# A decoder step on one core: decode strips queued as sets, keys before values in the projections, the convolution's norm earlier

## The chip, the cores and the metric

The kernel runs on one core of one Trainium2 chip. The time is the device time of one execution in microseconds (us). TensorE (PE) multiplies matrices, VectorE (DVE) and ScalarE (ACT) do elementwise work, GpSimd (POOL) too; SyncE (SP) issues every DMA. Each engine takes its instructions in order.

## What is computed

The reference runs one inference step of a trunk of two layers for a prompt of 1024 tokens and a sample group of 8 sequences with 4 new tokens each. The first layer mixes by differential attention (4 heads) beside a causal depthwise convolution of width 31, the second by a diagonal state-space scan; a squared-ReLU MLP stands behind each. Only the first layer's mixer is touched:

```python
def even_mixer(xn, w_in, lam_qk, subln_g, conv_w, conv_b, ln_g, ln_b, w_out, layer, k_past, v_past, conv_buf):
    q, k, v, ug = jnp.split(xn @ w_in, [A_Q_W, 2 * A_Q_W, 2 * A_Q_W + A_V_W], axis=-1)
...
    attn = rms_norm(attn, subln_g, SUBLN_EPS) * (1.0 - lam_init)
    a, g = jnp.split(ug, 2, axis=-1)
    u = a * jax.nn.sigmoid(g)
    c, new_buf = causal_depthwise_conv(u, conv_buf, conv_w, conv_b)
    c = jax.nn.silu(layer_norm(c, ln_g, ln_b))
    mixed = jnp.concatenate([attn.reshape(bt, L, A_V_W), c], axis=-1)
    return mixed @ w_out, k, v, new_buf
```

The prompt attends to itself. The sample group attends to 2048 cached tokens per sequence, in pages of 128 that a page table names, and to its own 4.

## The kernel before, in words

Activations lie with features on the 128 partitions and the 1056 tokens (1024 of the prompt, 32 new) on the free axis, as slabs of 128x1056 from a pool of 48; a pool of PSUM banks takes the products. Float32 operands are split in a high and a low part, and a product of 128x352 is three matmuls (L195 to L197). The code is emitted in program order with a scheduler behind it that sets each engine's order; DMAs keep the order of the program (`dma`, L96), on SP's one queue.

`mixer0` (L1488) computes 20 units of 128 features of the input projection in the order `seq` (L1491), `part` for a third of the tokens and `whole` (L1559) at the end of a unit: gates and conv inputs, queries, at the end values (8 to 11), then keys (4 to 7). Queries and keys are written to DRAM (`qd`, `kd`) and come back per head (`head_load`, L1281); `head_split` makes their high and low parts. `tokens` (L1475) transposes keys and values to tokens on the partitions, for the outputs and, values only, for `vd`, from which each head's values (`v`) are loaded.

Then `prompt` (L1431) runs 32 blocks, 4 heads by 8 blocks of 128 queries: scores (`sp`, L1324 to L1327), softmax in pieces (`pst`, `p`), transposed weights (`wT`, L1386), and with values (`av`, L1401). At block TH (24) it starts `conv_half`.

Beside this main line run generators, kept in `bg` and advanced by `pump` at given rates as the main line is emitted:

- `decode_k` (L1126) loads key pages (`pg`), transposes them (`kT`, L1142) and multiplies them with the new tokens' queries in *strips*: products of 32 rows that lie side by side on TensorE, one for each of 4 sequences (s) and 4 heads (h) (`strips`, `sc`, L1154). After 64 pages it waits for the new keys (`kready`), scores them and gives the group g (0 or 1) to `dec_softmax` (L1244), whose weights are transposed (`pT`).
- `decode_v` (L1191) loads value pages and multiplies, again in strips, four sequences side by side (`O`, L1217).
- `convs` (L981) computes the convolution on VectorE, 31 steps for each of 4 slabs (L977), and writes each slab (`acc`) to `cd`.
- `conv_norm` (L1037) runs when the projections have ended: it loads the four slabs, subtracts the mean over the 512 channels, sums squares, and multiplies by the root (`rows_rsqrt`, L1022: ScalarE's Abs_reciprocal_sqrt, `cs`); then Silu, and back to `cd`.
- `conv_half` (L1078) loads these (`cz`), splits them (`zh`, `zl`) and computes the conv half of the out-projection: 24 products of 12 matmuls.

Behind the last block the rest of `conv_half` and the attention's half of the out-projection follow (`finish`: `aT`, transposed heads; then `product`).

## Time and profile before

| | |
|---|---|
| runs | 2707.85, 2715.56, 2710.91 us; median 2710.91 |
| profiled execution | 2710.83 us, its span 2709.1 us |
| mean granted clock of TensorE | .967 |
| busy: PE, DVE, ACT, POOL | 2524.2, 1709.3, 1016.9, 738.3 us |
| projections of the first layer | 127 to 334 us |
| attention, blocks 1 to 20 | 333.7 to 496.8 us |
| attention, blocks 21 to 32 | 496.8 to 587.8 us |
| last score to `product` | 587.8 to 658.5 us |

Times are counted from the span's start. The profile is of one execution: the page gives sums over the whole span, in which TensorE is busy 93%; what a change in one stretch is worth is read from the rows of that stretch alone, in windows, waits (what ended an engine's idle time), groups of instructions, and the timeline. A matmul on 256 or 512 columns in float32 strips leaves two records. Ends of matmuls are modelled and overlap, so the time of one is read from its start to the next start.

### The profile page before, as it was taken

The page shows a single profiled execution, that of the slowest core. Times are in us where ns is not written, and L with a number is a line of the kernel's source. Part 1 is how long each engine was busy: PE and PEld are TensorE (multiplying, and loading weights), DVE is VectorE, ACT ScalarE, POOL GpSimd, SP SyncE. Part 2 cuts the span into 40 slices and gives each one's busy share as a digit, 9 for nine tenths or more (in the row PEclk, how much of TensorE's full clock was granted, in tenths as well). Part 3 has the DMA queues.
Part 4 walks back from the last instruction along what each step waited for, and adds up shares of the span by engine and source line. Part 5 has one row for each costly group of instructions (what it writes and reads, how often), then busy time and mean ns, then how long its engine had stood idle before and what let it go on. Part 6 is the DMA issues. An engine that isn't in the chain of part 4 may idle for free. (4 is left out here: it accounts for less than half of the span.)

```text
span 2709.1 us, 42679 instructions
## 1 busy us (share of the span) xinstructions
PE 2524.2 (93%) x16315; PEld 2392.4 (88%) x16315; DVE 1709.3 (63%) x3036; ACT 1016.9 (38%) x2034; POOL 738.3 (27%) x1090
## 2 busy tenths in 40 slices
PE   8999979789899999999999787799879999999998
PEld 7999855559799999999999776699779999999997
DVE  6777666763868554655545999951686767455435
ACT  6133345754441222222213466642552333412103
POOL 0110001112616875343402588710510000000004
PEclk9999989999999999999999899899889999999999
DMA  5353689663032223222222433213032233433221
GB/s 187 93 170 112 202 269 318 188 222 106 14 113 63 91 82 96 61 79 82 90 78 67 168 111 111 67 35 125 22 128 95 96 116 132 174 95 110 87 80 65
DMA packets 240868, 311.41 MB, mean 115 GB/s; under 512 B 27604, under 2 KB 168162, under 8 KB 240655
## 3 DMA queue, kind: packets, MB, share of 16 engines
q1 hardware_dynamic: 240331, 308.44, 35.3%
q8 instruction: 129, 2.11, 0.3%
q14 instruction: 76, 0.62, 0.1%
q10 hardware_dynamic: 332, 0.23, 0.0%
HBM read 235.33 MB, written 73.72 MB: 114 GB/s over the span
## 5 line engine op out<-in xcount | busy, mean ns | idle before, releaser
L195 PE MATMUL mm<-hh,whi 128*128 128x352 f32 x1536 | 498.2, 326 | 0.0
L197 PE MATMUL mm<-hh,wlo 128*128 128x352 f32 x1536 | 496.6, 323 | 0.0
L196 PE MATMUL mm<-hl,whi 128*128 128x352 f32 x1536 | 496.3, 323 | 0.0
L195 PE MATMUL mm<-zh,whi 128*128 128x352 f32 x1344 | 447.3, 334 | 0.2 <-ACT zh L218 0.2
L196 PE MATMUL mm<-zl,whi 128*128 128x352 f32 x1344 | 439.8, 327 | 3.2 <-DVE zl L219 3.2
L197 PE MATMUL mm<-zh,wlo 128*128 128x352 f32 x1344 | 437.3, 326 | 0.0
L293 POOL TENSOR_TENSOR ssq<-ssq,sq 128x352 f32<-128x352 f32 x72 | 72.8, 1011 | 935.6 <-ACT sq L292 934.8
L189 DVE TENSOR_TENSOR wlo<-wraw,whi 128x1024 fp32r<-128x1024 f32 x152 | 194.7, 1284 | 168.7 <-ACT whi L188 158.6
L196 PEld LDWEIGHTS mm<-hl,whi 128*128 128x128 f32 x1536 | 289.4, 188 | 0.5 <-issue 0.2
L195 PEld LDWEIGHTS mm<-hh,whi 128*128 128x128 f32 x1536 | 289.1, 188 | 0.6 <-issue 0.2
L197 PEld LDWEIGHTS mm<-hh,wlo 128*128 128x128 f32 x1536 | 289.1, 188 | 0.0
L188 ACT CAST whi<-wraw 128x1024 fp32r<-128x1024 f32 x152 | 158.6, 1047 | 284.2 <-DMA wraw<-in_w_ffn_down 153.8
L196 PEld LDWEIGHTS mm<-zl,whi 128*128 128x128 f32 x1344 | 257.0, 191 | 7.2 <-DVE zl L219 4.0
L195 PEld LDWEIGHTS mm<-zh,whi 128*128 128x128 f32 x1344 | 256.8, 191 | 5.8 <-issue 3.0
L197 PEld LDWEIGHTS mm<-zh,wlo 128*128 128x128 f32 x1344 | 256.8, 191 | 0.1
L597 DVE TENSOR_TENSOR y<-y,mm 128x352 f32<-128x352 f32 x312 | 155.1, 517 | 76.8 <-PE mm L197 74.9
L563 ACT ACTIVATE t<-t 128x352 f32<-128x352 f32 x96 | 47.7, 498 | 318.5 <-DVE t L562 318.5
L195 PE MATMUL mm<-xh,whi 128*128 128x352 f32 x480 | 160.5, 336 | 4.2 <-DVE xr L281 4.2
L774 DVE TENSOR_TENSOR y<-y,mm 128x352 f32<-128x352 f32 x144 | 74.9, 521 | 136.5 <-PE mm L197 136.5
L977 DVE SCALAR_TENSOR_TENSOR acc<-proj,keep,acc 128x1024 f32<-128x1024 f32 x120 | 156.3, 1303 | 3.0
L196 PE MATMUL mm<-xl,whi 128*128 128x352 f32 x480 | 157.1, 328 | 0.0
L197 PE MATMUL mm<-xh,wlo 128*128 128x352 f32 x480 | 157.1, 328 | 0.0
(533 smaller groups left out, 5532.9 us busy)
## 6 DMA issues: line engine op xcount, KB each, us to landing
pg<-in_cache_k SPq DMA_DIRECT2D x128, 256.0 KB
pg<-in_cache_v SPq DMA_DIRECT2D x128, 256.0 KB
wraw<-in_w_ffn_down SPq DMA_DIRECT2D x64, 512.0 KB
wraw<-in_w_ffn_up SPq DMA_DIRECT2D x36, 512.0 KB
hr<-hid SPq DMA_DIRECT2D x32, 528.0 KB
wq<-in_w_ffn_up SPq DMA_DIRECT2D x28, 512.0 KB
hres<-res SPq DMA_DIRECT2D x24, 528.0 KB
res<-y SPq DMA_DIRECT2D x24, 528.0 KB
```

Source lines behind the costliest of these rows:

```text
L188: nc.scalar.copy(hi[:, :n], raw[:, :n])
L189: (eng or nc.vector).tensor_sub(lo[:, :n], raw[:, :n], hi[:, :n])
L195: nc.tensor.matmul(out, wh, xh, start=first, stop=False)
L196: nc.tensor.matmul(out, wh, xl, start=False, stop=False)
L197: nc.tensor.matmul(out, wl, xh, start=False, stop=last)
L293: (nc.vector if k in YV else nc.gpsimd).tensor_add(s, s, q)
L563: nc.scalar.activation(t1, t1, AF.Square)
L597: nc.vector.tensor_add(yc, yc, pt)
L774: nc.vector.tensor_add(yc, yc, pt)
L977: nc.vector.scalar_tensor_tensor(acc[:, :NP], u[:, i:i + NP], w[:, k, i:i + 1], acc[:, :NP], op0=ALU.mult, op1=ALU.add)
```

## The change

- `together` puts the strips of a set behind the first of them in the scheduler's order; `strips` and `decode_v` use it.
- In `seq` keys now come before values; head 0 is loaded after the first key unit (its q and k alone) and split two units on. `values_load` loads a head's values at its block i == 1; the transposes of the values are advanced at rate 1.0, and finished there.
- The scores of the new keys are made as soon as `kready` is set (`fresh`), no longer awaited at the group's end; `decode_v` waits for the values' last tokens (`vready`).
- The convolution runs at rate 0.85 instead of 0.7. `conv_norm` starts at the end of the projections, keeps the last slab on chip, subtracts the mean straight from PSUM, sums squares on POOL, puts the variance on the token axis (10 small products), takes the root there by Newton steps on VectorE (`root`), and spreads it by diagonals (10 products).
- TH is 20: `conv_half` starts at block 20.

The diff, with some small places left out:

```diff
         return i
+    def together(self, products):
+        products = iter(products)
+        first = next(products)()
+        with self.tc.issue_after(first.ins):
+            for p in products:
+                p()
...
 LAM = 0.8 - 0.6 * math.exp(-0.3 * 0)
-TH, RC, RE = 24, 1.0, 1.0
+TH, RC, RE = 20, 1.0, 1.0
 KA, SL = 1, 1.0
-CV, CN, DL = 0.7, 1.0, 5.0
+CV, CN, DL = 0.85, 1.0, 5.0
...
                 nc.gpsimd.tensor_add(s, s, a)
-            self.dma(cd[k], a)
-            a = None
+            if k < 3:
+                self.dma(cd[k], a)
+                a = None
         while not self.projected:
             yield 1.0
-        self.bg_add(self.conv_norm(s, cd), CN)
+        gen = self.conv_norm(s, a, cd)
+        next(gen)
+        self.bg_add(gen, CN)
...
-    def conv_norm(self, s, cd):
-        nc = self.nc
-        acc = [self.S("acc") for _ in range(4)]
-        for k in range(4):
+    def conv_norm(self, s, last, cd):
+        nc = self.nc
+        acc = [self.S("acc") for _ in range(3)]
+        for k in range(3):
             self.dma(acc[k], cd[k])
+        acc.append(last)
+        last = None
         yield DL
-        q, r = self.S("cq"), self.S("cr")
         for c in range(NCH):
...
             nc.tensor.matmul(pt[:, :CH], self.ones.bitcast(F32), s[:, chunk(c)], start=True, stop=True)
-            nc.scalar.activation(r[:, chunk(c)], pt[:, :CH], AF.Copy, scale=1.0 / 512)
-            yield 0.6
-        for k in range(4):
-            nc.vector.tensor_sub(acc[k], acc[k], r)
-            nc.scalar.activation(s if k == 0 else q, acc[k], AF.Square)
-            if k:
-                nc.vector.tensor_add(s, s, q)
-            yield 2.5
-        yield 4.0
-        yield from self.rows_rsqrt(s, T, 512, r)
-        for k in range(4):
-            nc.vector.tensor_mul(acc[k], acc[k], r)
-            yield 2.0
+            for k in range(4):
+                a = acc[k][:, chunk(c)]
+                nc.vector.scalar_tensor_tensor(a, pt[:, :CH], -1.0 / 512, a, op0=ALU.mult, op1=ALU.add)
+                yield 0.6
+        s = None
+        rows = [b for c in range(NCH) for b in blocks(c)]
+        pt = self.PS("vs")
+        sq = self.S("cq")
+        nc.scalar.activation(sq, acc[0], AF.Square)
+        for k in range(1, 4):
+            q = self.S("cr")
+            nc.scalar.activation(q, acc[k], AF.Square)
+            nc.gpsimd.tensor_add(sq, sq, q)
+            yield 2.4
+        q = None
+        for i, (t, n) in enumerate(rows):
+            nc.tensor.matmul(pt[:n, i:i + 1], sq[:, t:t + n], self.ones.bitcast(F32)[:, 0:1], start=True, stop=True)
+        sq = None
+        yield 2.0
+        m = self.V(48)
+        x, y, t_ = (m[:, 16 * j:16 * j + 10] for j in range(3))
+        nc.vector.memset(m, 1.0)
+        x3, p3 = (z[:, 0:9].rearrange("p (c i) -> p c i", i=3) for z in (m, pt))
+        for n, v, q in ((P, x3[:, :, 0:2], p3[:, :, 0:2]), (96, x3[:, 0:2, 2:3], p3[:, 0:2, 2:3]), (64, m[:, 8:9], pt[:, 8:9]),
+                        (NS, m[:, 9:10], pt[:, 9:10])):
+            nc.vector.tensor_scalar(v[:n], q[:n], 1.0 / 512, 1e-5, op0=ALU.mult, op1=ALU.add)
+        self.root(x, y, t_)
+        yield 3.0
+        for c in range(NCH):
+            rb = self.PS("rb")
+            for t, n in blocks(c):
+                i = rows.index((t, n))
+                dg = self.H("t")[:, :P]
+                nc.vector.tensor_scalar(dg[:n, :n], self.ident[:n, :n], y[:n, i:i + 1], None, op0=ALU.mult)
+                nc.tensor.matmul(rb[:, t - c * CH:t - c * CH + n], self.ones.bitcast(F32)[:n, :], dg[:n, :n], start=True, stop=True)
+            yield 1.0
+            for k in range(4):
+                a = acc[k][:, chunk(c)]
+                nc.vector.tensor_mul(a, a, rb[:, :CH])
+                yield 0.6
         for k in range(4):
...
         self.normed = True
+    def root(self, x, y, t):
+        nc = self.nc
+        nc.vector.tensor_copy(t, x.bitcast(I32))
+        nc.vector.tensor_scalar(t, t, -0.5, 1597463007.0, op0=ALU.mult, op1=ALU.add)
+        nc.vector.tensor_copy(y.bitcast(I32), t)
+        for _ in range(3):
+            nc.vector.tensor_mul(t, y, y)
+            nc.vector.tensor_mul(t, t, x)
+            nc.vector.tensor_scalar(t, t, -0.5, 1.5, op0=ALU.mult, op1=ALU.add)
+            nc.vector.tensor_mul(y, y, t)
...
         def strips(sc, g, cols, rhs):
-            for h in range(4):
-                for s in range(4):
-                    nc.tensor.matmul(sc[32 * s:32 * s + 32, cols], qs[:, h, 4 * g + s, :], rhs(s, h), start=h == 0, stop=h == 3)
+            self.together((lambda h=h, s=s: nc.tensor.matmul(sc[32 * s:32 * s + 32, cols], qs[:, h, 4 * g + s, :], rhs(s, h),
+                                                             start=h == 0, stop=h == 3))
+                          for h in range(4) for s in (3, 0, 1, 2))
+        held = []
+        def fresh():
+            while held and self.kready:
+                g, SA, SB = held.pop(0)
+                sc = self.PS("sc")
+                strips(sc, g, slice(0, NS), lambda s, h: ks[:, 32 * h:32 * h + 32])
+                nc.vector.tensor_add(SB[:, NP:T], sc[:, :NS], self.nmask[g])
+                self.bg_add(self.dec_softmax(g, SA, SB), 1.0)
...
             if pr == 7:
-                while not self.kready:
-                    yield 1.0
-                sc = self.PS("sc")
-                strips(sc, g, slice(0, NS), lambda s, h: ks[:, 32 * h:32 * h + 32])
-                nc.vector.tensor_add(SB[:, NP:T], sc[:, :NS], self.nmask[g])
-                yield 0.5
-                self.bg_add(self.dec_softmax(g, SA, SB), 1.0)
+                held.append((g, SA, SB))
+            fresh()
+        while held:
+            yield 1.0
+            fresh()
...
         load, raw = self.pages("v")
-        while not self.ready:
+        while not (self.ready and self.projected and self.vready):
             yield 1.0
...
                 w = PT[kt // 8][:, kt % 8, :]
-                for e in range(4):
-                    nc.tensor.matmul(O[32 * e:32 * e + 32, :], w[:, 32 * e:32 * e + 32], pgs[e][:, 512 * j:512 * j + 512],
-                                     start=False, stop=kt == 15)
+                self.together((lambda e=e: nc.tensor.matmul(O[32 * e:32 * e + 32, :], w[:, 32 * e:32 * e + 32],
+                                                            pgs[e][:, 512 * j:512 * j + 512], start=False, stop=kt == 15))
+                              for e in (3, 0, 1, 2))
                 yield 2.0
...
-    def head_load(self, h, qd, kd, vd):
-        q, v = self.S("q"), self.S("v")
+    def head_load(self, h, qd, kd):
+        q = self.S("q")
         k = [self.S("k") for _ in range(2)]
...
                 self.dma(k[c][64 * e:64 * e + 64, :NP], kd[h, 64 * c:64 * c + 64, :NP])
-        vv = v[:, :1024].rearrange("p (i d) -> p i d", i=8)
-        self.dma(vv, vd[:NP, h * P:(h + 1) * P].rearrange("(i p) d -> p i d", p=P))
-        return q, k, v
-    def head_split(self, q, k, v):
+        return q, k
+    def values_load(self, h, vd):
+        v = self.S("v")[:, :1024].rearrange("p (i d) -> p i d", i=8)
+        self.dma(v, vd[:NP, h * P:(h + 1) * P].rearrange("(i p) d -> p i d", p=P))
+        return v
+    def head_split(self, q, k):
...
                 if i == 3 and h < 3:
-                    raw[h + 1] = self.head_load(h + 1, qd, kd, vd)
+                    raw[h + 1] = self.head_load(h + 1, qd, kd)
+                if i == 1:
+                    for _ in self.vgen:
+                        pass
+                    V[h] = self.values_load(h, vd)
                 if i == 0:
...
                 pcs[t] = []
-                yield from self.scores(i, hd[h][:2], st, hs[h], pcs[t])
+                yield from self.scores(i, hd[h], st, hs[h], pcs[t])
                 if i == 7 and h < 3:
...
                 if i % 2:
-                    self.values(i, Ws.pop((h, i // 2)), hd[h][2], at[h], hs[h])
+                    self.values(i, Ws.pop((h, i // 2)), V[h], at[h], hs[h])
                     yield 0.33 * (i + 1)
                 if i == 7:
-                    del hd[h]
+                    del hd[h], V[h]
                     self.bg_add(self.head_norm(at[h], hs[h]), SL)
...
         win = a["w_in_even"][0]
-        seq = [16, 12, 17, 13, 0, 1, 2, 3, 18, 14, 19, 15, 8, 9, 10, 11, 4, 5, 6, 7]
+        seq = [16, 12, 17, 13, 0, 1, 2, 3, 18, 14, 19, 15, 4, 5, 6, 7, 8, 9, 10, 11]
         wt, out = {}, {}
...
                     self.dma(kd[h], d)
-                    if h == 1:
-                        first.append(self.head_load(0, qd, kd, vd))
+                    if h == 0:
+                        first.append(self.head_load(0, qd, kd))
                     if h == 2:
...
                 elif m == 11:
-                    self.bg_add(self.tokens(list(kv), T, put_v), 0.2)
+                    self.vgen = self.tokens(list(kv), T, put_v)
+                    self.bg_add(self.vgen, 1.0)
                     kv.clear()
...
                 nc.scalar.copy(vS[:NS, :], st[:NS, :512])
+                self.vready = True
...
         first = []
+        self.weights, self.ready = [], False
         ahead = [self.gains(["g_mix_post", "g_ffn_pre", "g_ffn_post"]), self.consts0(), self.conv_state()]
...
             prep(i + 2)
+            if i == 12:
+                self.lam()
             if i == NX + 4:
...
         at = []
-        self.lam()
-        self.weights, self.ready = [], False
         self.projected = True
```

TensorE, inside the attention's first blocks, before: one set of 16 key strips (`sc` out of `kt` and the queries `QB`) stands in pieces between scores (`sp`), page transposes (`kT`) and value strips.

```order
L1154 MATMUL sc_4283<-kt_4251,QB_895 32x256
L1324 MATMUL sp_4396<-kh__595_4211,qp_4210 128x256
L1325 MATMUL sp_4396<-kl__596_4212,qp_4210 128x256
L1327 LDWEIGHTS keep_589
L1327 MATMUL sp_4396<-keep_316,keep_589 128x128
L1324 MATMUL sp_4400<-kh__598_4218,qp_4217 128x256
L1325 MATMUL sp_4400<-kl__599_4219,qp_4217 128x256
L1327 LDWEIGHTS keep_589
L1327 MATMUL sp_4400<-keep_316,keep_589 128x128
L1142 MATMUL kT_4419<-ident,pg_4243 128x128 x4
L1154 MATMUL sc_4283<-kt_4338,QB_895 32x256
```

The same place after:

```order
L1391 MATMUL sp_4554<-keep_316,keep_589 128x128
L1203 MATMUL sc_4307<-kt_4434,QB_896 32x256
L1203 MATMUL sc_4307<-kt_4242,QB_896 32x256
L1203 MATMUL sc_4307<-kt_4392,QB_896 32x256
L1203 MATMUL sc_4307<-kt_4413,QB_896 32x256
```

These four follow each other three times more, and then a `wT` comes: the set stands in one run of 16. Of the value strips nearly all stand in runs of four or more.

TensorE, some five blocks after the start of `conv_half` (blocks 25 to 32), after the change:

```order
L1465 MATMUL av_6230<-v_5536,wT_6045 128x128 x4
L203 MATMUL mm_6291<-zh_5737,whi_5763 128x352
L204 MATMUL mm_6291<-zl_5738,whi_5763 128x352
L205 MATMUL mm_6291<-zh_5737,wlo_5761 128x352
...
L205 MATMUL mm_6291<-zh_5949,wlo_5761 128x352
L1388 MATMUL sp_6306<-kh__931_6031,qp_6030 128x384
```

Runs of 12 matmuls of `conv_half` (`mm` out of `zh`, `zl` and the weights' `whi`, `wlo`) now stand between the attention's values (`av`) and scores, 132 matmuls ahead of the last score; before there were none. Between the last values and the first `aT` there are now 80 of them.

SP's queue at the start of the attention, after:

```order
L96 DMA pg_3480<-in_cache_k 128x512
L96 DMA out_new_v_prompt<-tok_3500 128x512
L96 DMA vd<-tok_3500 128x512
...
L96 DMA out_new_v_sample<-tok_3587 32x512
L96 DMA v_3591<-vd 128x8x128
L96 DMA acc_3615<-cd 128x1056
L96 DMA acc_3616<-cd 128x1056
L96 DMA acc_3617<-cd 128x1056
...
L96 DMA pg_3637<-in_cache_k 128x512
...
L96 DMA pg_3652<-in_cache_v 128x512
```

The writes of new values, eight pairs in all (`tok` holds a block of tokens) and one of the sample's, now stand with the load of head 0's values and three loads of conv slabs between the key pages 75 and 76 and the first value pages; before, the writes of values stood in the projections, and here were those of the keys, without `vd`.

## Rows read from the trace of the kernel before

**Rows 1.** Windows of the profile, core 0: window, us, busy us (count) of each engine, granted clock, DMA share, GB/s.

```profile
333.70:496.80 163.10, 138.76 (x1073) 94.75 (x1072) 111.28 (x264) 86.69 (x227) 9.69 (x22) 0.94 0.90 289
496.80:587.80 91.00, 69.43 (x450) 43.83 (x450) 64.65 (x174) 63.99 (x157) 15.59 (x42) 0.91 0.62 203
587.80:658.50 70.70, 66.57 (x423) 58.88 (x423) 26.83 (x46) 33.37 (x73) 8.86 (x21) 1.00 0.34 103
```

**Rows 2.** Windows, the same columns, for DMA.

```profile
356.00:500.00 144.00, 130.01 (x999) 86.16 (x997) 92.63 (x225) 75.59 (x203) 9.29 (x31) 0.96 0.96 306
500.00:530.00 30.00, 18.66 (x135) 15.13 (x139) 21.64 (x62) 22.60 (x59) 5.44 (x12) 0.89 0.23 70
```

**Rows 3.** Timeline of SP's DMA queue: start us, us, queue, line, DMA, count.

```profile
356.36 13.86 SPq L96 DMA_DIRECT2D pg<-in_cache_v  x14
...
484.40 1.70 SPq L96 DMA_DIRECT2D pg<-in_cache_k  x2
```

**Rows 4.** What TensorE waited for, blocks 1 to 20: total us, times, longest.

```profile
PE wT L1386 <- DVE p L1372: 12.9, 4, 6.6
PE kT L1142 <- DMA pg<-in_cache_k: 7.7, 2, 7.5
```

**Rows 5.** What TensorE waited for, blocks 21 to 32 and just behind.

```profile
PE wT L1386 <- DVE pst L1365: 5.0, 1, 5.0
PE sp L1325 <- DVE kl__900_5905 L219: 4.1, 1, 4.1
PE wT L1386 <- DVE pst L1335: 2.6, 1, 2.6
```

**Rows 6.** Groups of TensorE instructions, last stage: count, busy us, mean ns, idle before.

```profile
L195 PE MATMUL mm<-zh,whi 128*128 128x352 f32 x97 | 32.5, 335 | 0.2 <-ACT zh L218 0.2
L196 PE MATMUL mm<-zl,whi 128*128 128x352 f32 x96 | 31.1, 324 | 0.0
L197 PE MATMUL mm<-zh,wlo 128*128 128x352 f32 x96 | 31.0, 323 | 0.0
```

**Rows 7.** Timeline of TensorE, strips and what follows them: start us, us, count of records.

```profile
219.02 1.94 PE L1154 MATMUL sc<-kt,QB 128*32 128x256 f32 x32
220.89 0.61 PE L1009 MATMUL cvo<-ident,proj 128*30 128x128 f32 x4
...
383.34 1.47 PE L1142 MATMUL kT<-ident,pg 128*128 128x128 f32 x12
384.75 0.62 PE L1154 MATMUL sc<-kt,QB 128*32 128x256 f32 x2
385.30 0.44 PE L1267 MATMUL pT<-ident,SB 128*128 128x128 f32 x2
...
592.83 1.05 PE L1217 MATMUL O<-pg,PT 128*32 128x512 f32 x2
593.80 0.43 PE L196 MATMUL mm<-zl,whi 128*128 128x352 f32 x1
...
614.23 1.06 PE L1217 MATMUL O<-pg,PT 128*32 128x512 f32 x8
615.22 0.43 PE L195 MATMUL mm<-zh,whi 128*128 128x352 f32 x1
```

**Rows 8.** Groups of VectorE from 333.7 to 355, of ScalarE from 500 to 550, and the page's.

```profile
L977 DVE SCALAR_TENSOR_TENSOR acc<-proj,keep,acc 128x1024 f32<-128x1024 f32 x9 | 11.4, 1272 | 0.0
...
L1030 ACT ACT_TABLE_LOAD x3 | 3.8, 1283 | 0.1
...
L774 DVE TENSOR_TENSOR y<-y,mm 128x352 f32<-128x352 f32 x144 | 74.9, 521 | 136.5 <-PE mm L197 136.5
```

**Rows 9.** Windows of 10 us, columns as in the first group.

```profile
334.00:344.00 10.00, 3.37 (x54) 2.87 (x53) 9.59 (x26) 5.40 (x13) 0.00 (x0) 0.85 0.44 159
344.00:354.00 10.00, 7.89 (x50) 6.50 (x48) 10.00 (x19) 5.54 (x14) 2.42 (x1) 0.81 0.42 134
354.00:364.00 10.00, 8.35 (x47) 7.88 (x51) 5.37 (x17) 6.39 (x17) 0.00 (x0) 0.66 1.07 261
```

More of the change, by code (lines that the diff above doesn't have):

```diff
@@ L921, in consts0 @@
         nc.vector.tensor_scalar(self.subg, self.cv[:, 0:1], LAM - 1.0, None, op0=ALU.mult)
-        nc.vector.tensor_scalar(self.cv[:, 5:9], self.cv[:, 5:9], -1.0, None, op0=ALU.mult)
         self.eps5 = self.C([P, 1], "eps5")
@@ L1305, in head_split @@
             K.append((kh, kl))
-        return Q, K, v[:, :1024].rearrange("p (i d) -> p i d", i=8)
+        return Q, K
     def scores(self, i, qk, st, hs, pc):
@@ L1431, in prompt @@
     def prompt(self, first, qd, kd, vd, at, when, then):
-        raw, hd = {}, {0: first}
+        raw, hd, V = {}, {0: first}, {}
         blk = [(h, i) for h in range(4) for i in range(8)]
@@ L1516, in mixer0 @@
         tiles, kv, u = [], [], []
-        self.normed = self.projected = self.kready = False
+        self.normed = self.projected = self.kready = self.vready = False
         def part(i, c, pt=None):
```

## The prediction

> **What bounds the kernel now.** The profiled execution took 2710.83 us, 0.1 us from the median of the runs, so sums against it need no shift. Measurement tells about 0.3% (8 us) from no change. I read first the windows of the stretch that the change touches, then the DMA of the same stretch, then what TensorE waits for, and last the timeline of single strips. Two stages lie there: attention, whose first scores start at 333.7, and the out-projection behind its last scores (587.8), up to the product at 658.5.
>
> Blocks 1 to 20 (333.7 to 496.8): TensorE is busy 138.8 of 163.1 us [rows 1], so it looks like the bound. But from 356 to 500 the DMA engines are at a share of .96 and move 306 GB/s [rows 2]: 44 MB, mostly cache pages, go through SP's one queue, from the first value pages (issued from 356.4) to the last key pages (484.4 to 486.1) [rows 3]. The last keys then need some 11 us more on TensorE, which ends block 20 at 496.8. **The page stream sets that end**; TensorE's idle time, the largest pieces being 12.9 us for the softmax's p on VectorE and 7.7 us for key pages [rows 4], is slack against it.
>
> Blocks 21 to 32 (496.8 to 587.8): TensorE is busy 69.4 of 91.0 us [rows 1] while DMA has little to do at first (70 GB/s from 500 to 530) [rows 2]. Its longest waits end with VectorE: 5.0 and 2.6 us for pst (the softmax's sums and maxima), 4.1 for kl (the split keys of the next head) [rows 5]. Here the chain scores, softmax, wT, av sets the pace and **TensorE has holes**.
>
> Last score to product (587.8 to 658.5): busy 66.6 of 70.7 at a clock of 1.00 [rows 1]. TensorE alone is the bound; 289 of its instructions are the out-projection's products (97, 96 and 96 by line) [rows 6].
>
> **Part 1, strips as sets.** A whole set of 16 key strips (32 records) starts at 219.02 and the next work at 220.89: 1.87 us. A lone strip (two records) at 384.75 takes 0.55, five times its 0.117 in a set. A lone value strip at 592.83 takes 0.97, four together at 614.23 take 0.99 [rows 7]. Adding up start to next start over the timeline, the 128 key strips of the attention take 20.4 us; as 8 whole sets 15.0: 5.4 less. Value strips take 21.0 in blocks 1 to 20 (17 packs at .92 are 15.6), 18.8 in 21 to 32 and 6.7 behind them. The new order keeps nearly all whole.
>
> **Part 2, keys before values in the projections.** Sixteen key transposes more stand ahead of the first score (280, before 264). Twelve take 1.41 us at 383.34 [rows 7], so these 1.9. The scores of the new keys, which come ahead too, cost 0.4; one set less is broken, -0.6. Eight writes of new keys pass SP ahead of two pages: 2.1 MB at 306 GB/s [rows 2] is 7 us, covered by the pages loaded ahead; without this cover up to 7.5, the longest wait for key pages seen [rows 4]. I take the cover as whole: **+1.7** for the start of the attention, bounds -1 and +9. That the attention has fewer transposes left gives nothing back, since they lie in the page-bound stretch.
>
> **Part 3, head 0 split and conv done earlier.** Nine conv steps of 1.27 us sit on VectorE between 333.7 and 355 [rows 8]; all move ahead of the first scores. They are most of the longest wait for p, 6.6 us [rows 4]. But the values' path comes to that place: 36 transposes, 17 writes (4.2 MB, 13.7 us at 306 GB/s), then the load of v, the conv's three and two key pages stand on SP ahead of the first value pages. Transposes done at some 10 us, writes by 22 to 24: the value pages start as late as before, 22.6 us into the attention. From there to the last key page 38.9 MB go instead of 39.8: 126.5 instead of 129.4 us. With the 11 us behind it, block 20 would end 160 to 161 us after the first scores; with a little more queueing 162, against 163.1: **-1.3**. What VectorE and the strips free in this stretch becomes waiting for pages. Bounds: -18, were TensorE's own work the bound (138.8 - 5.4 - 5.4 + some 5 for the norm's 20 products and the values' four more transposes + 12 idle = 145), and +10, if pages come late at the start.
>
> **Part 4, conv norm.** On ScalarE three root evaluations go, with their table loads of 1.28 us, three ahead of the roots between 500 and 550 [rows 8], and as many back to the softmax's table; on VectorE some 20 tiny operations, 10 diagonals and 12 subtractions on 128x352 come in, these 12 at about the 0.52 of the eviction of that size [rows 8], all in blocks 4 to 16, whose end the pages set; POOL takes the sums of squares. Nothing of it is on the path; were that cover gone, its 4 us of TensorE work would be. What it buys is the time at which the out-projection's conv half may begin.
>
> **Part 5, conv half from block 20 instead of 24.** Before, not one of its products stands ahead of the last score; now 132 of 288 do, between blocks 25 and 32. A product takes 0.168 (48.2 us for 287 in the timeline of the last stage). Of the 91.0 us of blocks 21 to 32, 69.4 are work [rows 1]; 5.0 of it go with whole sets (15 packs at .92 for 18.8), and 4.0 because the norm's sums and the new keys' scores now stand earlier. The products add 132 x 0.16, as long as they stand in dense runs: 21.1, so 81.5 of work. The holes ahead of block 25 (5.0 and 2.6 for pst [rows 5], and small ones) have no filler and stay: some 8.6. The other 13 us of holes are filled: 81.5 + 8.6 = 90.1, **-1**, bounds -6 and +8. Eleven more evictions of 0.52 us [rows 8] on VectorE lie beside its 64.7 us of 91 [rows 1].
>
> Last stage: 132 x 0.168 = 22.2 leave; 14 value strips in six runs (6.7 us) become two packs (1.9): -4.8; idle -1: **-28**, bounds -20 and -30. aT still has 80 products as cover for the last head's norm, where there were 108.
>
> **Behind it** TensorE's order is the same for thousands of products; a few exchange places in the odd layer: 0, bounds -5 and +5.
>
> Sum: +1.7 - 1.3 - 1 - 28 = -28.6: **2682 us**.
>
> **A rule against it.** From 354 to 364 the granted clock is .66, a stretch partly at 1.2 and partly at 2.4 GHz; TensorE had been busy for 7.9 of the 10 us ahead of it and, before the 6.6 us wait for p ended at 343.35, for 3.4 of 10 [rows 9]. The Trainium skill, "TensorE: Matmul & The Clock Gate", section "Loop structure matters more than you think", says that waiting for a DMA ahead of each group of matmuls lets the clock fall to half. By it, a faster TensorE in a page-bound stretch would only wait more often and run colder. This is in rival b.
>
> **Rivals.**
> (a) *TensorE, not pages, ends block 20.* For it: 138.8 busy of 163.1 [rows 1]. Against: share .96 with 306 GB/s [rows 2]. Then strips count in full: about -16 more, 2666.
> (b) *Pages late at the start, clock low.* The new queue puts 17 writes, v and the conv's loads ahead of the key and value pages that blocks 3 to 8 need, and those blocks now ask for pages earlier (key transposes stand six further by block 6). Each wait of the kind in rows 4 costs up to 7.5. Were the granted clock .80 from 356 to 500 instead of .96 [rows 2], 126 us of work would be 151, with 12 idle about 8 more than the stretch has. Together +10 to +17: 2695.
> (c) *Value pages become the bound in blocks 25 to 32: slower.* The conv half holds eight operand slabs, weights and results from block 20, out of the 48 that the value pages also need; TensorE is in order, so one late page holds scores and filler alike. A late page costs up to 7.5 [rows 4]; eleven packs stand in these blocks. From four late packs on (30 us) the gain is gone; at six, +45 - 29 = +16: 2727. Against: DMA has room from 500 to 530, 70 GB/s [rows 2].
> (d) *The filler doesn't fill.* The products stretch blocks 25 to 32 by their whole 22 us, since softmax steps queue behind their evictions. Then only the strips at the end and a few us remain: -9, 2702.
>
> **How the numbers follow.** Forecast .55, its own range 2672 to 2691; a .12, b .17, c .06, d .08, anything else .02. The range 2662 to 2703 takes in the forecast, a and b, and of d about half: some .85 of the chance, shaded for costs that I don't see. Faster (under 2702.8): .55 + .12 + .17 + .04 = .88. Same: half of d and the rest, .06. Slower: c, .06.
>
> **What would show it.** The profile after should have: key strips only in runs of 32 records; no conv step on VectorE behind the first score; block 20 some 162 us behind the first scores with DMA share still above .9; 132 products between blocks 25 and 32 and PE busy near 81 of 90 there; last score to product near 42 us. A stretch to block 20 under 155 us speaks for a; waits for pages above 15 us in the first 50 and a clock under .8 for b; waits for value pages behind block 25 for c; blocks 21 to 32 over 105 us for d. The prediction is wrong if the last stage shrinks by less than 20 us, or what it loses comes back ahead of it.

## The result, and the profile after

The changed kernel takes 2678.11 us (median of six runs, 2676.12 to 2682.2), the one before 2709.38 in the same rounds: a ratio of 0.9885, interval 0.9872 to 0.9897. Forecast were 2682 and a range of 2662 to 2703. The profiled execution has a span of 2677.1 us, 32.0 less than before.

Windows of the profile after, cut at the places of [rows 1]: first score, first score of block 20, last score, product, and the first product out of the MLP's hidden values (hh) behind it (columns as there). Blocks are counted from 1, TH counts from 0. The cut called the end of block 20 ahead of the prediction is the first score of block 20, which before stands at 496.0, 0.8 us ahead of the cut in [rows 1]; so block 20 itself lies in the stretch called blocks 21 to 32, before and after alike, and the table takes 496.0, 587.6 and 658.3 for before.

```profile
127.00:325.90 198.90, 193.91 (x1474) 182.33 (x1473) 150.82 (x144) 71.45 (x126) 20.49 (x15) 0.99 0.53 168
325.90:484.30 158.40, 130.89 (x1122) 93.59 (x1121) 107.88 (x294) 89.45 (x227) 16.79 (x29) 0.92 0.95 314
484.30:576.40 92.10, 79.99 (x530) 59.48 (x529) 64.72 (x175) 55.93 (x159) 14.88 (x37) 0.96 0.60 192
576.40:621.40 45.00, 39.52 (x279) 37.11 (x279) 19.24 (x34) 24.93 (x54) 7.30 (x21) 0.99 0.39 122
621.40:754.70 133.30, 117.75 (x670) 114.99 (x670) 92.75 (x144) 58.22 (x123) 55.58 (x51) 0.91 0.22 75
```

| stretch | forecast | before to after, us | change |
|---|---|---|---|
| start of the attention | +1.7 | 333.7 to 325.9 | -7.8 |
| blocks 1 to 20 (to the first score of 20) | -1.3 | 162.3 to 158.4 | -3.9 |
| blocks 21 to 32 | -1 | 91.6 to 92.1 | +0.5 |
| last score to product | -28 | 70.7 to 45.0 | -25.7 |
| behind it | 0 | 2050.8 to 2055.7 | +4.9 |
| sum | -28.6 | | -32.0 |

So the total was right, and the largest term nearly so; the start and the part behind were off most, in opposite directions. Stretch by stretch:

**Blocks 1 to 20.** DMA runs at a share of .95 with 314 GB/s from the first score on; before it came to .96 and 306 only from 356 on [rows 2], and to .90 and 289 over the whole stretch [rows 1]. SP issues the first value pages from 346.43 and has the last key pages out at 468.96, 122.5 us later; before, 129.7 lay between (356.36 to 486.10 [rows 3]). SP's timeline after (start, length, count of issues):

```profile
341.80 0.37 SPq L96 DMA_DIRECT2D v<-vd  x1
342.26 1.48 SPq L96 DMA_DIRECT2D acc<-cd  x3
344.49 1.23 SPq L96 DMA_DIRECT2D pg<-in_cache_k  x2
346.43 11.18 SPq L96 DMA_DIRECT2D pg<-in_cache_v  x14
464.31 4.65 SPq L96 DMA_DIRECT2D pg<-in_cache_k  x6
469.74 0.86 SPq L96 DMA_DIRECT2D pg<-in_cache_v  x2
```

What TensorE waited for in this stretch after (as [rows 4]):

```profile
PE wT L1450 <- DVE p L1436: 17.4, 4, 13.9
PE kT L1193 <- DMA pg<-in_cache_k: 5.3, 2, 4.7
```

The longest wait for p did not go; it grew from 6.6 to 13.9 us. VectorE's timeline shows why: the norm's first subtractions stand at conv slabs that are still on the way (issued at 342.26, above, behind the values' writes), and the next softmax is queued behind them:

```profile
346.86 0.53 DVE L1062 SCALAR_TENSOR_TENSOR acc<-cs,acc 128x352 f32<-128x352 f32 x1 [9.85 <-DMA acc<-cd]
349.12 0.53 DVE L1062 SCALAR_TENSOR_TENSOR acc<-cs,acc 128x352 f32<-128x352 f32 x1 [1.74 <-DMA acc<-cd]
350.85 0.96 DVE L1062 SCALAR_TENSOR_TENSOR acc<-cs,acc 128x352 f32<-128x352 f32 x2 [1.20 <-DMA acc<-cd]
351.72 0.68 DVE L1396 TENSOR_REDUCE pst<-sp 128x1 f32<-128x512 f32 x1
```

**Last stage.** A new wait stands just ahead of the product: 5.5 us, until ScalarE has squared the decoded attention; that square had queued behind five casts of MLP weights. TensorE's timeline (last products of the conv half, sums, first products), then ScalarE's:

```profile
615.17 0.32 PE L205 MATMUL mm<-zh,wlo 128*128 128x352 f32 x1
620.97 0.80 PE L1039 MATMUL cs<-sq,ones 128*128 128x128 f32 x2 [5.48 <-ACT sq L1537]
621.42 0.64 PE L203 MATMUL mm<-zh,whi 128*128 128x352 f32 x1
621.86 0.49 PE L204 MATMUL mm<-zl,whi 128*128 128x352 f32 x1
615.88 4.83 ACT L196 CAST whi<-wraw 128x1024 fp32r<-128x1024 f32 x5
620.61 0.31 ACT L1537 ACTIVATE sq<-keep 128x128 f32<-128x128 f32 x1
```

Behind the wait a matmul of the product takes 0.29 us from start to start (621.86 to 622.15 in the next row) instead of 0.16: the granted clock is .66 from 620 to 630. From its first to its last matmul the product takes 41.9 us, 39.0 before: 2.9 of the +4.9 arise here. The whole window to the first product out of hh is 3.7 us longer (133.3 after, 129.6 before).

### The profile page after: what moved, and what is told of

It is laid out like the page before. It is cut to its first block, busy times and chain, and to the rows that moved or that the text cites. A ratio compares the mean times of both kernels' runs of the same rounds, so it can differ in the third digit from the quotient of the medians.

```text
span 2677.1 us, 42789 instructions
## 1 busy us (share of the span) xinstructions
PE 2497.3 (93%) x16349; PEld 2384.9 (89%) x16349; DVE 1713.5 (64%) x3070; ACT 1006.0 (38%) x2022; POOL 754.6 (28%) x1093
```

## The experiments

Eleven runs; "stages" are read from each profile at the same scores and products. Kernels that are the same up to the attention start it at 324 to 332 us in their profiles, so stage lengths say more than single totals. A profile is of one execution, and some lie well off the median of their kernel: strips one by one 8.4 us above it, sets alone 6.4 above, conv half from block 24 6.0 above, decode's norm first 4.4 below, the norm 25 us later 7.9 below. An effect of a few us on the total is told by the medians only where the intervals part.

**More bytes on the queue.**

```diff
     def head_load(self, h, qd, kd):
-        self.dma(q[:, :NP], qd[h, :, :NP])
+        for _ in range(2 if h in (1, 2) else 1):
+            self.dma(q[:, :NP], qd[h, :, :NP])
...
```

> The changed kernel with the queries and keys of heads 1 and 2 loaded twice: 3.1 MB more on SP's queue ahead of block 20, no work more on any other engine. If the page stream sets the end of block 20 (A), it comes 7 to 10 us later (3.1 MB at 314 GB/s): 2685 to 2688. If the engines' own chain sets it (B): 0 to 3 us, 2678 to 2681.

Measured: 2687.44, ratio 0.9914 (0.9898 to 0.9931). Blocks 1 to 20 take 171.3 instead of 158.4 us, 12.9 more where 7 to 10 were expected; the two value pages behind the last key pages go out at 482.96, 138 us behind the first ones at 345.01, instead of 123.3 (346.43 to 469.74):

```profile
324.50:495.80 171.30, 136.77 (x1124) 94.67 (x1122) 108.95 (x295) 89.25 (x227) 16.72 (x30) 0.91 0.94 305
356.02 2.39 SPq L96 DMA_DIRECT2D k<-kd  x4
362.83 0.34 SPq L96 DMA_DIRECT2D q<-qd  x1
482.96 0.86 SPq L96 DMA_DIRECT2D pg<-in_cache_v  x2
```

The two stages behind are within 1 us of those after (92.9 and 44.9). No compute engine got more work, and block 20 came later by more than the bytes take: SP's stream of loads sets that end. A is right here, B falls. The bytes do not stand alone, though. A second load writes the same tile as the first, and SP stood 4.4 us behind the first loads before it issued the second ones (358.41 to 362.83 in the rows), 4.6 us for the other head; its waits for q came to 8.9 us, 2.5 after. How much of the 12.9 is bytes and how much is the held queue, this run does not tell.

**The norm's subtractions later.**

```diff
         yield DL
+        yield 6.0
```

> The changed kernel with the conv norm's subtractions emitted some 6 us later, so that VectorE no longer stands at them while their slabs are on the way, with the softmax queued behind. The 13.9 us wait of TensorE for p in block 3 goes. Theory A (the page stream sets the end of block 20): that end moves by less than 3 us, 2678 becomes 2675 to 2679. Theory B (TensorE's chain sets it): 9 to 13 us earlier, 2665 to 2669.

Measured: 2687.57, ratio 0.9910 (0.989 to 0.993): slower, which neither theory had; the intervals touch, but all four runs lie above all six of the changed kernel. The wait of 13.9 is gone, and block 5 begins 9 us earlier (23.4 us after the first score, not 32.6). By block 6 most of this is lost (43.7 and 44.7), to key pages:

```profile
PE kT L1194 <- DMA pg<-in_cache_k: 8.1, 1, 8.1
PE wT L1451 <- DVE p L1437: 3.8, 3, 1.6
PE vs L1077 <- POOL cq L1073: 3.5, 1, 3.5
PE av L1466 <- DMA v<-vd: 3.4, 1, 3.4
PE O L1277 <- DMA pg<-in_cache_v: 2.7, 1, 2.7
PE rb L1095 <- DVE t L1094: 2.7, 1, 2.7
```

So far as A says, and block 12 still comes 4 us earlier (95.1 and 99.3). But then blocks 12 to 20, where the norm now stands, take longer: the sums wait 3.5 us for POOL (vs), the spread 2.7 for VectorE (rb). Waits of 0.6 us and more add up to 11.5 us from there on, 4.1 after. Block 20 comes at 165.8 us, 7.4 later, though the pages had all been issued as early as after (141.9 us behind the first score, 143.8 after). So the stream sets the end of block 20 only as long as the engines keep up behind it; here they did not. That in blocks 4 to 16 the norm stood in waits that pages would have filled anyhow is a reading, not shown by a run of its own.

**Strips one by one, and sets alone.** The first kernel is the changed one with the loops of before in `strips` and `decode_v`, the second the kernel before with `together` and the order 3, 0, 1, 2.

```diff
-            self.together((lambda h=h, s=s: nc.tensor.matmul(sc[32 * s:32 * s + 32, cols], qs[:, h, 4 * g + s, :], rhs(s, h),
...
-        with self.tc.issue_after(first.ins):
...
```

> The changed kernel with the strips queued one by one again (in the order 0 to 3, nothing held behind the latest): 27 runs of key strips instead of 16, 35 runs of value strips instead of 25. Theory A (the page stream sets the end of block 20): the strips' 5 us in blocks 1 to 20 stay hidden; some 1.5 us more in the projections, 2 to 3 in blocks 21 to 32: 2678 becomes 2681 to 2684. Theory B (TensorE's own work sets block 20): another 5 to 7 us there, 2687 to 2692.

> The kernel before with the strips queued as sets and nothing else changed: 19 runs of key strips (before 34), 23 of value strips (34). If the page stream sets the end of block 20 (A): 1.5 to 2 us less in the projections, 0 to 3 in blocks 1 to 20, 2 to 4 in blocks 21 to 32, 4 to 5 in the last stage, where the value strips stand in packs: 2709 becomes 2696 to 2701. If TensorE's own work sets it (B), another 5 to 8: 2689 to 2694.

Measured: strips one by one 2684.91, ratio 0.9900 (0.9879 to 0.9922), stages +3.2, +4.3 and +0.9 from the first score on, against the changed kernel. The total lies 1 us above what A expected and 2 below B, and its interval overlaps the changed kernel's, so it does not decide between them. In blocks 1 to 20 the 3.2 lies between them too (0 and 5 to 7), but it is a quarter of what TensorE works more there (142.9 us, 130.9 after): the larger part stays hidden. Sets alone 2705.85, ratio 0.9983 (0.9972 to 0.9994): 4.6 us, where A expected 8 to 13 and B more, so both missed. In the changed kernel a whole set takes 1.86 us (336.48 to 338.34), as in [rows 7]. The profile of the kernel with sets alone is of an execution that gained nothing (2712.26), so it cannot show where the median's 4.6 us arose; it shows how the work saved can be lost:

```profile
335.90:495.40 159.50, 130.29 (x1064) 94.19 (x1063) 109.84 (x263) 87.06 (x227) 10.09 (x24) 0.91 0.89 293
495.40:590.70 95.30, 68.77 (x453) 45.41 (x451) 65.04 (x176) 65.52 (x160) 14.67 (x40) 0.84 0.61 198
```

In blocks 21 to 32 TensorE works 68.8 us instead of 70, at a clock of .84 instead of .91 ([rows 1] give .91), and the stretch is 95.3 us long, not 91.6. In this execution shorter work there went with longer waits and a lower clock.

**When the conv half starts.** The second kernel has 28 for 24.

```diff
-TH, RC, RE = 20, 1.0, 1.0
+TH, RC, RE = 24, 1.0, 1.0
```

> The changed kernel with the out-projection's conv half started at block 24 as before: 48 of its matmuls instead of 132 stand ahead of the last score. Theory A (the products fill holes, which cost time with or without them): blocks 21 to 32 keep about 91 us, and the last stage takes 84 x 0.165 = 14 us more: about 2691, less what the better covered wait ahead of the product gives back (2686 to 2692). Rival (the products stretch the blocks by what they take): blocks 21 to 32 shrink by 10 to 14 us, and the time stays at 2678 (2675 to 2681).

> The changed kernel with the conv half started at block 28, which puts none of its matmuls ahead of the last score, as it was before the change (108 ahead of the first aT). If the 132 matmuls ahead of the last score fill holes (forecast): blocks 21 to 32 shrink by at most 4 us, the last stage takes 22 more, less 7 for the wait ahead of the product that then has cover: 2688 to 2692. By the rate of the run with block 24 (84 matmuls worth 2 us): blocks 21 to 32 shrink by 7 to 9, and 2680 to 2683.

Measured: block 24: 2679.78, ratio 0.9881 (0.986 to 0.9903), the same as the changed kernel; block 28: 2693.25, ratio 0.9933 (0.9917 to 0.995), 15 us slower. The first total is in the rival's range, but not for the rival's reason: blocks 21 to 32 shrank by 3.8 us, not 10 to 14, and the last stage grew by 7.4, not 14. The second is 1 us above the forecast's range, with the last stage 22.0 longer as that had it, and the blocks 7.4 shorter as the other line had it. Windows of blocks 21 to 32 and of the last stage, for block 24, then for block 28:

```profile
489.40:577.70 88.30, 71.73 (x448) 51.14 (x447) 63.81 (x173) 51.42 (x147) 16.18 (x37) 0.86 0.62 202
577.70:630.10 52.40, 52.40 (x363) 50.27 (x363) 22.08 (x37) 28.97 (x62) 7.29 (x21) 1.00 0.35 106
484.80:569.50 84.70, 65.42 (x400) 44.23 (x399) 58.59 (x168) 49.46 (x143) 14.66 (x37) 0.84 0.61 202
569.50:636.50 67.00, 62.41 (x412) 59.63 (x411) 25.43 (x44) 31.16 (x67) 9.92 (x21) 0.97 0.30 91
```

| matmuls ahead of the last score | blocks 21 to 32 | clock | last stage |
|---|---|---|---|
| 0 (block 28) | 84.7 | .84 | 67.0 |
| 48 (block 24) | 88.3 | .86 | 52.4 |
| 132 (block 20, changed kernel) | 92.1 | .96 | 45.0 |

The first 48 shorten the last stage by 14.6 us for 3.6 in the blocks; 4.6 of the 14.6 is idle time that only the kernel with block 28 has there. The next 84 give 7.4 and cost 3.8, and 1.3 more behind the product, for the new wait has then lost its cover: with block 24 the last stage has no idle time at all. So the forecast's chain (holes filled, last stage shorter by what moves) holds as a whole, but its second half is worth 2 us.

TensorE's groups show how the blocks took 22.7 us of products in 7.5. With none of them (block 28), then after:

```profile
L1465 PE MATMUL av<-v,wT 128*128 128x128 f32 x92 | 14.8, 328 | 0.0
L1450 PE MATMUL wT<-ident,p 128*128 128x128 f32 x56 | 11.2, 335 | 15.3 <-DVE p L1436 10.2 <-DVE pst L1429 5.0
```

```profile
L1465 PE MATMUL av<-v,wT 128*128 128x128 f32 x92 | 12.7, 297 | 0.0
L1450 PE MATMUL wT<-ident,p 128*128 128x128 f32 x56 | 9.4, 292 | 9.0 <-DVE p L1436 9.0
```

The same 92 `av` take 328 ns each without products, 297 with them, the `wT` 335 and 292, and the wait for p falls from 10.2 to 9.0 and that for pst (5.0) goes. By start to next start, all work but the products falls from 65.3 to 57.3 us, idle time from 19.3 to 12.1: **half of the room came from the clock, half from holes.** An estimate from the granted clocks agrees: 65.3 us at .84 would be 57.1 at .96. The Trainium skill, "TensorE: Matmul & The Clock Gate", section "Loop structure matters more than you think", shows a long wait for a DMA ahead of a matmul turning the engine cold. Here the waits are for VectorE, and filling a part of them brought the clock from .84 to .96.

**Where and in which form the norm stands.** Both start from the kernel with block 28, which has no products in these blocks: first the new norm emitted 25 us later (diagonals and Silu in blocks 22 to 25, as before), then the old form in the new place.

```diff
         yield DL
+        yield 25.0
```

> The kernel with the conv half behind (conv half from block 28, none of its matmuls ahead of the last score), with the conv norm emitted 25 us later, so that its diagonals and Silu stand in blocks 22 to 25 as the old norm did. If the norm's place is what made blocks 21 to 32 as long as 92 us before (theory now): these blocks take 91 to 95 us instead of 84.6, blocks 1 to 20 stay within 3 us, and 2693 becomes 2699 to 2704. Rival (the sets or the norm's new form shortened these blocks): 84 to 87 us, 2691 to 2696.

> The kernel with the conv half behind, with the old form of the norm (four slabs loaded, mean by ScalarE, roots by ScalarE with their table loads, products over whole slabs) in the new place, blocks 5 to 15. If the place decides: within 3 us of the kernel with the conv half behind, 2690 to 2697, since the page stream sets the end of block 20 anyhow; the 0.5 MB more on SP's queue cost 2 us of that. If the form decides (no table loads, less work on VectorE): blocks 1 to 20 take 5 to 10 us more, 2698 to 2703.

Measured: 2699.5, ratio 0.9956 (0.9942 to 0.9971), and 2696.61, ratio 0.9948 (0.9928 to 0.9968). Blocks 21 to 32:

```profile
482.70:566.60 83.90, 64.14 (x419) 42.90 (x418) 64.08 (x201) 54.77 (x145) 16.85 (x42) 0.90 0.66 228
493.80:576.40 82.60, 64.55 (x398) 42.26 (x396) 59.80 (x176) 50.15 (x143) 16.86 (x42) 0.86 0.62 206
```

83.9 and 82.6 us, against 84.7: in these executions neither place nor form alone makes them 92 or 95 us long. By the stages the theory that the norm's place did falls, and the rival's 84 to 87 comes closest. Old form in old place, with sets, is the kernel with sets alone (95.3), which has other differences too (32 records of key strips still stand behind block 20 there); which of them decides was not separated. The second lies within what the place theory expected for it, with blocks 1 to 20 at 161.6, 3.5 us longer; the first's median, 2699.5, is 6 us higher than that of the kernel with block 28 and lies in the theory's range. Its profile does not show why: it is of the shortest of the eight runs (2691.61; they reach to 2703.28), and there every stage behind the first score is as long as with block 28. The five longer runs (2699.4 and more) have mean granted clocks of .962 to .964, the three shorter ones .967 to .970; none of the longer ones is profiled, so whether the norm's place has a part in them stays open.

**Values before keys.**

```diff
-        seq = [16, 12, 17, 13, 0, 1, 2, 3, 18, 14, 19, 15, 4, 5, 6, 7, 8, 9, 10, 11]
+        seq = [16, 12, 17, 13, 0, 1, 2, 3, 18, 14, 19, 15, 8, 9, 10, 11, 4, 5, 6, 7]
```

> The changed kernel with the old order of units at the projections' end (values, then keys; rest as changed). If keys first gave the shorter projections (some 6 us of 207), they grow by 4 to 6 us; on the other side the values' writes no longer delay the conv slabs at the start of the attention, and the 13.9 us wait in block 3 goes, which gives at most 3 us: 2679 to 2684. Rival (projections are shorter for whole sets, fewer page waits and the warmer clock behind them, whatever the order): projections within 2 us of the changed kernel's, 2673 to 2679.

Measured: 2675.68, ratio 0.9866 (0.9849 to 0.9882), no slower than the changed kernel. The total is in the rival's range, but the stages are as neither line had them: the attention starts at 339.3, 13 us later, and blocks 1 to 20 take 148.8 us, 10 less: their end lies at 488.1, after 484.3. Of the 13, 9.3 us are one wait in the projections: strips for their keys' copy, queued on ScalarE behind the cast of the last unit's weights, whose load SP had queued behind head 0's, and that behind the landing of a key unit:

```profile
300.82 3.64 PE L1203 MATMUL sc<-kt,QB 128*32 128x256 f32 x32 [9.30 <-ACT kt L1196]
```

Some of the rest lies ahead of the projections: from 20 to 60 us the granted clock is .87 in this profile, .96 after.

**The decode's norm first.**

```diff
-        self.ffn_early(0, 2)
         self.drain()
...
         for _ in self.subln(av, P):
             pass
+        self.ffn_early(0, 2)
```

> The changed kernel with the norm of the decoded attention emitted ahead of the first MLP weights' preparation, so that its square on ScalarE no longer queues behind five casts. If these casts cause the 5.5 us wait just ahead of the product, and the half clock behind it, 6 to 8 us go: 2670 to 2672. Rival: the product's first operands wait for something else by then (the new tokens' part of the operands on VectorE, or the first sums), and the first gap behind the product grows by as much: 2676 to 2679.

Measured: 2676.28, ratio 0.9877 (0.9855 to 0.9899). The wait shrinks from 5.5 to 1.7 us, the last stage from 45.0 to 41.0, and the stretch behind by 1.1:

```profile
PE cs L1039 <- ACT sq L1537: 1.7, 1, 1.7
```

The casts were the cause of that wait. Of the 7 us that the profile shows (span 2670.1, the shortest of the four runs), the medians show 2, in the rival's range and not in the 6 to 8 us expected; the runs spread over more than the difference, so what the wait is worth in the total is not shown.

**The combination.**

```diff
-                    if h == 0:
+                    if h == 1:
                         first.append(self.head_load(0, qd, kd))
-                    if h == 2:
+                    if h == 3:
                         first[0] = self.head_split(*first[0])
```

with values before keys and the decode's norm first.

> The changed kernel with the decode's norm first (as run on its own), values before keys, and head 0 loaded after the second key unit and split after the fourth. In the run with values first the last unit's weights landed 10 us late, behind a load that waits for the keys' write, which cost 9.3 us and a cold clock in the projections; the start of the attention was 10 us shorter. Without that wait: projections 200 to 205 us, blocks 1 to 20 149 to 154, product 4 us earlier: 2664 to 2670. Rival (the page stream alone sets the end of block 20, wherever the projections end): that end stays at 482 to 486 us from the start, and only the 2 to 4 us of the decode's norm are won: 2673 to 2676.

Measured: 2671.24 (2669.15 to 2673.15), ratio 0.9858 (0.9837 to 0.9878):

```profile
127.00:332.40 205.40, 194.27 (x1431) 181.85 (x1430) 142.85 (x135) 66.91 (x120) 18.57 (x15) 0.98 0.51 168
332.40:483.90 151.50, 136.71 (x1151) 97.36 (x1152) 112.93 (x301) 92.73 (x230) 16.96 (x30) 0.93 0.92 302
483.90:577.00 93.10, 81.56 (x531) 61.35 (x531) 64.83 (x175) 56.21 (x160) 14.45 (x37) 0.95 0.67 214
577.00:618.10 41.10, 39.41 (x280) 37.01 (x279) 15.22 (x31) 20.87 (x49) 7.27 (x21) 1.00 0.29 87
```

The projections take 205.4 us, the blocks 151.5, close to or in the ranges of the first line; block 20 begins at 483.9, as after (484.3), which is the rival's picture. The total lies between the two, 1 us above the first range and 2 below the rival's, and decides for neither. Its four runs all lie under all six of the changed kernel, taken in other rounds; the two intervals against the kernel before overlap, so that this version is the faster of the two is likely and not shown to the last.

## Why the prediction was right, and where it was off

That the total came so near is luck in part: the start came 9.5 us lower than its term, the part behind 4.9 higher, and the blocks and the last stage made up smaller differences both ways.

- **Start of the attention** (+1.7, was -7.8). The cover held, and the sixteen transposes cost 0.8 us (31.5 for 280, against 30.7 for 264). The step that failed is the bound of -1: the sum put at nothing the waits that the old order had. Before, key pages stood behind the values' writes and the load of head 0 on SP, and TensorE waited 4.0 us for them; the rows of before, the window of the projections, SP and then TensorE:

```profile
127.00:333.70 206.70, 197.38 (x1430) 184.97 (x1429) 136.45 (x131) 68.47 (x119) 14.70 (x14) 0.96 0.51 165
298.32 0.37 SPq L96 DMA_DIRECT2D kd<-proj  x1
298.78 0.41 SPq L96 DMA_DIRECT2D q<-qd  x1
299.24 2.68 SPq L96 DMA_DIRECT2D k<-kd  x4
301.98 0.58 SPq L96 DMA_DIRECT2D v<-vd  x1
303.33 8.14 SPq L96 DMA_DIRECT2D pg<-in_cache_k  x8
311.90 1.08 PE L1142 MATMUL kT<-ident,pg 128*128 128x128 f32 x4 [3.96 <-DMA pg<-in_cache_k]
```

  Waits of TensorE in the projections fell from 9.3 to 5.0 us, the mean clock rose from .96 to .99 (3.0 us on the same products), and whole sets gave 1.8. These three are 9.1 less, the costs 0.8 and 0.4. The two profiles have nearly the same clock ahead of the projections (.95 and .96 from 20 to 60 us), so the difference is not of the kind told in the last section. No run changes the order alone without another wait coming in, so this account is read from the two profiles and not shown by a run.
- **Blocks 1 to 20** (-1.3, was -3.9): the page stream as the bound, shown by the loads added to SP's queue; the norm moved later shows its limit. The time from first value pages to last key pages was forecast at 126.5 and is 122.5, the pages start 20.5 us behind the first score (22.6), and 15.3 us follow the last key pages (11): the terms were off both ways, and their sum is near by luck. That rival a would be worth 16 us more is excluded: TensorE's work did fall by 7 us (138 to 130.9), and its idle time grew by 3.
- **What was thought to give nothing** (the wait of 6.6 for p, "most of" it from conv steps): the steps left, and the conv slabs' loads took their place on the same engine, with 13.9. Rival b had the loads in its queue and no engine behind them; the stretch did not grow for it. The clock fell from .94 to .92, far from the .80 it priced; and its price does not follow from its rows, for 151 us of work and 12 idle are 163, 19 more than the 144 from 356 to 500 and not 8.
- **Blocks 21 to 32** (-1, was +0.5): without products 84.7 us, as 81.5 - 21.1 of work and 21.6 of holes would give 82; with them 92.1. The step "the other 13 us of holes are filled" failed in kind: 7 were filled, and 8 came from the clock. That the products lengthen the blocks by 7.4 where the sum had 8.1 (82 to 90.1) is luck. Rival d's mechanism, stretching, is seen for 7.5 of 22 us.
- **Last stage** (-28, was -25.7): value strips in packs 2.0 us (forecast 1.9), 132 products fewer 22.5 (22.2). Off is "idle -1": the 4.1 us of waits before went, but a square that had had cover lost it and brought 5.5, so idle time grew by 1.4.
- **Behind** (0, was +4.9): 2.9 of it is the product at the cold clock behind that wait. The rest is not explained by it: the kernel with block 28, which has no such wait, takes 2055.3 us from its product's start to the end, as much as after.
- Rival c, late value pages, did not come: no wait for value pages stands in blocks 21 to 32 after.

## What to carry to other kernels

Where a transfer stream sets a stretch's end, work of the engines there counts for only a part of its time (12 us more of TensorE's cost 3.2 with the strips one by one), so it is the place for what must be done anyhow, but not close to its end: there the norm cost 7.4. Adding loads and no other work tests whether a stream is the bound; here second loads that had to wait for the first blurred the size. Filler for an engine that waits for another's chain pays twice, in the hole and in the clock, and its last part pays least, for the tail behind loses its cover: look in each queue for what had been hidden (here five casts ahead of one small square). An order of units that shortens one stage may only move its waits into another while the stream behind both stays as it is.

## What was not expected of the hardware

The same instructions ran at other clocks for what stood between them: the 92 `av` matmuls took 328 ns or 297, at a granted clock of .84 or .96 over the stretch. And profiles of kernels with the same instructions up to the attention differ early on: from 20 to 60 us the clock was .96 in the profile after, and .87 in that of the conv half from block 24, where the attention starts at 331.0, not 325.9. Of the others the conv half from block 28, more bytes and the norm 25 us later have 1.00 there and start at 324 to 327, and the norm's subtractions later has .87 and starts at 329.0. What sets this clock is open:

```profile
20.00:60.00 40.00, 38.14 (x235) 35.60 (x234) 28.19 (x88) 27.43 (x54) 0.91 (x3) 0.96 0.46 138
20.00:60.00 40.00, 37.93 (x217) 35.11 (x216) 26.42 (x86) 24.93 (x47) 0.74 (x3) 0.87 0.48 139
```
